# Decoder layer on one core: w_out and the feed-forward weights loaded into one shared ring of tiles, and the last units of the down projection finished one by one

## The chip, the cores and the metric

The kernel runs on one core of a Trainium2 chip. Times are microseconds of device time. Below, PE is TensorE, DVE is VectorE, ACT is ScalarE, POOL is GpSimd and SP is SyncE, which here only issues DMAs.

## What is computed

One layer of a hybrid decoder for 2112 tokens (64 sample tokens and 2048 prompt tokens), model width 1024, hidden width 2816, all in fp32:

```python
m = concat(rms_norm(gla(x @ w_in)) * silu(gate), rms_norm(gdn(x @ w_in)) * silu(gate)) @ w_out
x = layer_norm(ALPHA * x + m)
hid = silu(x @ w_ffn_gate) * (x @ w_ffn_up)
y = layer_norm(ALPHA * x + hid @ w_ffn_down)
```

`gla` and `gdn` are two recurrences over chunks of tokens, whose last states are outputs too.

## The kernel before

**Precision.** Every fp32 matmul of the large products is made as three: each operand is split into a rounded high part h and a rest l, and PE adds up h·h, h·l and l·h in PSUM. A split is an ACT cast (h) and a DVE subtraction (l).

**Stages.** phase_in projects x by w_in. The mixing (phase_gla, phase_gdn) runs the two recurrences, whose results go to device memory (`on_d` for the head outputs, `gt_d` for the gates). It ends at about 1108.5 us of the span. phase_out (L1038) follows, with 17 units: unit 0 has 64 tokens, units 1 to 16 have 128. Then comes the feed-forward: the gate and up products run over 3 blocks of 704 tokens and 22 weight slices f (until about 2285 us), the down projection over 5 groups of 4, 4, 3, 3 and 3 units and 22 slices each.

**One unit of phase_out** (`project`, L1054). For both head groups, `on` and `gt` are loaded, ACT sums the squares of `on` (L1066), POOL makes the factor, DVE scales, PE transposes `on` into PSUM `pt` (L1073: four 128x128 transposes), DVE multiplies by the gate (tile `gt`), ACT casts the high part `oh` (L1078), DVE makes the rest `ol`. Then 48 matmuls with 512 columns multiply by w_out (`gemm_t`, L249 to L251): 24 into one PSUM tile `pw` for the left 512 output columns, 24 into another for the right ones. DVE adds the residual out of PSUM (`xt`, L1088), a layer norm follows, PE transposes the result (`px`, L1094, two times four), ACT copies each half out of PSUM into the tile `x1T` (L1096) and issues its DMA to device memory itself (L1100). The pool has one buffer of `x1T` (`X1T = 1`), so that the second copy can only be made when the DMA of the first has landed.

**w_out before.** `load_quad` (L166 or so, called at the start of phase_out) loads w_out in eight DMAs of 512 KB through a staging tile `wraw` with two buffers. On each, DVE multiplies by the gain of the norm in place (L173), ACT casts the high part (L174), DVE subtracts. The parts stand in `o0h`, `o0l`, `o1h`, `o1l`.

**The feed-forward's weights before.** `load_pair` loads one slice of gate and up in one DMA of 1 MB into `wr` (two buffers), POOL makes three sums (`wt`), and seven splits go to `w` (nine pairs). The first call stands behind all of phase_out. `seven` multiplies in seven products p of 12 matmuls with 352 columns per half block. The down projection loads two slices per DMA into the same `wr`.

**Order of the work.** The kernel is written as if instructions ran in turn. A scheduler, which simulates a timeline when the program is built, then sets the order of the instructions on each engine, and inside an engine that order is kept on the chip. The program gives its hardware-queued DMAs eight landing semaphores in turn. So an edit in one place can move instructions of other places, and the order is read from the built program.

**End.** In the last group of the down projection (units 14 to 16, 18 matmuls per slice f and group), the loop over f is outside and the loop over units inside, so all three units end with the last slice, and their additions, layer norms and stores (L1210 to L1213) come behind PE's last matmul. The last unit's layer norm uses DVE for its last step, others ACT and POOL (`spare`).

Of the kernel before, what the change touches and what calls it, by code (L numbers as in the profile page):

```python
# [18 lines left out]
D = 1024  # L19
# [81 lines left out]
def hybrid_layer(ctx: ExitStack, tc: tile.TileContext, I, O):  # L101
# [25 lines left out]
    def vtt(out, a, b, op):  # L127
        nc.vector.tensor_tensor(out, a, b, op=op)  # L128
# [31 lines left out]
    c_G = cols.tile([64, 4], F32, name="c_G")  # L160
    flag = cols.tile([1, 1], mybir.dt.int32, name="flag")

    stg = ctx.enter_context(tc.tile_pool(name="stg", bufs=2))
    psg = ctx.enter_context(tc.tile_pool(name="psg", bufs=2, space=PSUM))

    def load_quad(pool, tag, src, gain):  # L166

        wh, wl = (pool.tile([128, 8, 512], F32R, name=tag + p, tag=tag + p, bufs=1) for p in "hl")
        v = src.rearrange("(k p) c -> p k c", p=128)
        for k in range(0, 8, 2):  # L170
            raw = stg.tile([128, 2, 512], F32, name="wraw", tag="wraw", bufs=2)
            nc.sync.dma_start(out=raw, in_=v[:, k:k + 2, :])
            nc.vector.tensor_scalar(raw, raw, gain[:, k // 4:k // 4 + 1], None, op0=TT.mult)  # L173
            nc.scalar.copy(wh[:, k:k + 2, :], raw)  # L174
            vtt(wl[:, k:k + 2, :], raw, wh[:, k:k + 2, :].bitcast(F32), TT.subtract)
        return wh, wl

# [17 lines left out]
    def sums(raw_x, r):  # L195

        r["S3"], r["S2"], r["S4"] = raw_x(), raw_x(), raw_x()
        ptt(r["S3"], r["11"], r["21"], TT.subtract)
        ptt(r["21"], r["21"], r["22"], TT.add)
        r["S1"] = r["21"]  # L200
        ptt(r["S2"], r["S1"], r["11"], TT.subtract)
        ptt(r["S4"], r["12"], r["S2"], TT.subtract)
        return r

    def load_pair(pw, src, plain=False):
# [40 lines left out]
    def gemm_t(out, wh, wl, xs, ts):  # L246

        for k in range(8):
            nc.tensor.matmul(out, lhsT=xs[0][k][:, ts], rhs=wh[:, k, :], start=(k == 0), stop=False)  # L249
            nc.tensor.matmul(out, lhsT=xs[0][k][:, ts], rhs=wl[:, k, :], start=False, stop=False)  # L250
            nc.tensor.matmul(out, lhsT=xs[1][k][:, ts], rhs=wh[:, k, :], start=False, stop=(k == 7))  # L251

# [15 lines left out]
    def phase_in(stack):  # L268
# [83 lines left out]
        for ib in range(3):  # L352
# [3 lines left out]
            for p in range(6):  # L356
# [680 lines left out]

    def phase_out(stack, ffn):  # L1038
        pi, po, p3 = (stack.enter_context(tc.tile_pool(reuse_waits=RW, name=n, bufs=2, side="right"))
                      for n in ("pi", "po", "p3"))  # L1040
        psm = stack.enter_context(tc.tile_pool(reuse_waits=RW, name="pso", bufs=2, space=PSUM))
        gain = pi.tile([128, 2], F32, name="gain", bufs=1)
        nc.sync.dma_start(out=gain, in_=I["norm_g"])
        wo = [load_quad(po, f"o{i}", I["w_out"][:, 512 * i:512 * i + 512], gain) for i in range(2)]
        lng = p3.tile([128, D], F32, name="lng", bufs=1)
# [8 lines left out]
        def project(u):  # L1054
# [53 lines left out]

    def phase_ffn(stack):
        NF = DFF // 128  # L1110
        pa = stack.enter_context(tc.tile_pool(reuse_waits=RW, name="pa", bufs=2))

# [34 lines left out]
        yield  # L1147
        pw = stack.enter_context(tc.tile_pool(reuse_waits=RW, name="pw", bufs=2, side="right"))
        p4 = stack.enter_context(tc.tile_pool(reuse_waits=RW, name="p4", bufs=2, side="right"))
        psp = stack.enter_context(tc.tile_pool(reuse_waits=RW, name="psp", bufs=6, space=PSUM))  # L1150

        for ib in range(3):
            xs = load_x1(ib) if ib else x_first
            for f in range(NF):
                kept = {}

                def done(j, i, t):
# [3 lines left out]
                    if (1 - j, i) in kept:  # L1161
# [14 lines left out]
        for nu in (4, 4, 3, 3, 3):  # L1176
# [8 lines left out]
            ys = {}  # L1185
            for f in range(NF):
                if f % 2 == 0:
                    raw = pw.tile([128, 4, 512], F32, name="wr")
                    nc.sync.dma_start(out=raw, in_=I["w_dn"][f // 2])
                wd = [part(pw, "w", 9, [128, 512], raw[:, 2 * (f % 2) + i, :], 512) for i in range(2)]  # L1190
                hr = p4.tile([128, 512], F32, name="hr")
                nc.sync.dma_start(out=hr[:, :T], in_=hid_d[f][:, c0:c0 + T])
                hh, hl = part(p4, "h", 3, [128, 512], hr[:, :T], T)
                if f == 0:
                    for u in us:
                        ys[u] = p4.tile([128, D], F32, name="y", bufs=5)
                        nc.sync.dma_start(out=ys[u][:units[u][1]], in_=x1_d[u])
                for u in us:
                    u0, C = units[u]
                    ts = slice(u0 - c0, u0 - c0 + C)  # L1200
                    for i in range(2):
                        p = ps[u, i][:C]
                        nc.tensor.matmul(p, lhsT=hh[:, ts], rhs=wd[i][0], start=f == 0, stop=False)  # L1203
                        nc.tensor.matmul(p, lhsT=hh[:, ts], rhs=wd[i][1], start=False, stop=False)  # L1204
                        nc.tensor.matmul(p, lhsT=hl[:, ts], rhs=wd[i][0], start=False, stop=f == NF - 1)  # L1205
            for u in us:
                u0, C = units[u]
                for i in range(2):
                    sl = slice(512 * i, 512 * i + 512)
                    nc.vector.scalar_tensor_tensor(ys[u][:C, sl], ys[u][:C, sl], ALPHA, ps[u, i][:C],  # L1210
                                                   op0=TT.mult, op1=TT.add)
                layer_norm(p4, ys[u], C, lng, lnb, spare=u < 16)
                ST.dma_start(out=O["y"][u0:u0 + C, :], in_=ys[u][:C])  # L1213
        yield

    def finish(rest):
        ffn = phase_ffn(rest)
        with ExitStack() as stack:
            phase_out(stack, ffn)
        next(ffn)  # L1220
# [21 lines left out]

GT, X1T = 3, 1
DEEPEST = 24.0
PBK = {"sc": 1, "inv": 2, "seq": 2, "po": 1}
# [61 lines left out]
```

## Time and profile before

| what | us |
|---|---|
| median of three runs | 2833.39 |
| lowest and highest run | 2832.21, 2848.49 |
| the profiled execution | 2829.82 |
| its span in the profile | 2827.7 |
| PE busy in the span | 2665.6 (94%) |
| DVE, ACT, POOL busy | 1982.8, 1241.3, 1176.9 |

The span goes from the first to the last recorded instruction of the profiled execution; 2.1 us lie around it. Stretches named below are microseconds from the start of the span. PE's busy share is an average: idle time of PE stands in the mixing, in the first 35 us of phase_out, at the change to the feed-forward, and at the end. The granted clock (PEclk) is the share of full speed that TensorE's clock had; 1.00 is 2.4 GHz, 0.50 is 1.2 GHz.

### The profile page before, as it was taken

How to read it: one execution, taken by the hardware profiler on the slowest of the kernel's cores; microseconds unless marked ns; L12 is line 12 of the kernel's file. 1: busy time of each engine (PE TensorE's matmuls, PEld its weight loads, DVE VectorE, ACT ScalarE, POOL GpSimd, SP SyncE). 2: the span in 40 equal slices, each digit the busy share in tenths (PEclk: the TensorE clock that was granted, in tenths of full speed). 3: DMA queues.
4: the chain of work that ended last, by engine and by line, in shares of the span. 5: the costliest groups of instructions: out<-in, count | busy, mean ns of one | idle time of the engine just before them, and what ended most of it. 6: DMA issues, size and time to landing. Idle time of an engine off the chain costs nothing.

```text
span 2827.7 us, 45495 instructions
## 1 busy us (share of the span) xinstructions
PE 2665.6 (94%) x16362; PEld 2435.2 (86%) x16362; DVE 1982.8 (70%) x3160; ACT 1241.3 (44%) x2660; POOL 1176.9 (42%) x1185
## 2 busy tenths in 40 slices
PE   8999999997888887999799999999999999999996
PEld 8999999995767675777799999999999987887885
DVE  7868768655678766686677788777877743555664
ACT  5545445434455553343344453444444432334442
POOL 6534325324344431354555559655665500210111
PEclk9999999996899998999899999999999999999998
DMA  7345344324533223667732346323432243536652
GB/s 258 126 152 186 121 144 157 108 101 126 148 98 99 65 70 102 188 205 240 239 117 101 112 147 203 114 101 124 140 107 103 100 144 131 202 131 244 214 200 85
DMA packets 244232, 406.60 MB, mean 144 GB/s; under 512 B 27900, under 2 KB 202460, under 8 KB 223132
## 3 DMA queue, kind: packets, MB, share of 16 engines
q1 hardware_dynamic: 195900, 364.22, 39.0%
q10 hardware_dynamic: 48096, 39.38, 4.2%
q8 instruction: 131, 2.15, 0.3%
q14 instruction: 105, 0.86, 0.1%
HBM read 305.01 MB, written 98.51 MB: 143 GB/s over the span
## 4 chain that ended last, share of the span: by engine, by line
PE 48%; DMA 2%; DVE 2%; POOL 1%; issue 1%; ACT 0%; SPq 0%; POOLq 0%; ACTq 0%; DVEq 0%
PE p L227 10%; PE p L228 10%; PE p L226 10%; PE p L1203 4%; PE p L1205 4%; PE p L1204 4%; PE g L1203 2%; PE g L1205 2%; PE g L1204 2%; DMA x1T<-x1T 1%; DMA xr<-x1T 1%; POOL xr L131 1%; DVE xl L128 0%; DMA wr<-in_w_dn 0%; DVE wl L128 0%
## 5 line engine op out<-in xcount | busy, mean ns | idle before, releaser
L128 DVE TENSOR_TENSOR wl<-wr,wh 128x512 fp32r<-128x512 f32 x652 | 595.1, 916 | 337.8 <-ACT wh L182 335.4
L226 PE MATMUL p<-xh,wh 128*128 128x352 f32 x2520 | 814.3, 323 | 10.2 <-ACT x1T L1096 5.0
L227 PE MATMUL p<-xl,wh 128*128 128x352 f32 x2520 | 815.1, 323 | 4.1 <-DVE xl L128 4.1
L228 PE MATMUL p<-xh,wl 128*128 128x352 f32 x2520 | 814.4, 323 | 0.3 <-DVE wl L128 0.3
L182 ACT CAST wh<-wr 128x512 fp32r<-128x512 f32 x652 | 401.1, 620 | 582.1 <-PE p L227 274.8
L226 PEld LDWEIGHTS p<-xh,wh 128*128 128x128 f32 x2520 | 474.6, 188 | 11.6 <-ACT x1T L1096 5.4
L227 PEld LDWEIGHTS p<-xl,wh 128*128 128x128 f32 x2520 | 474.8, 188 | 5.9 <-DVE xl L128 5.6
L228 PEld LDWEIGHTS p<-xh,wl 128*128 128x128 f32 x2520 | 474.8, 188 | 0.8 <-DVE wl L128 0.8
L128 DVE TENSOR_TENSOR t<-t,p 128x352 f32<-128x352 f32 x630 | 318.7, 518 | 199.0 <-PE p L228 197.3
L131 POOL TENSOR_TENSOR wt<-wr 128x512 f32<-128x512 f32 x180 | 243.9, 1355 | 242.8 <-DVE wl L128 211.7
L182 ACT CAST wh<-wt 128x512 fp32r<-128x512 f32 x270 | 167.5, 621 | 311.7 <-PE p L227 280.5
L1028 POOL TENSOR_SCALAR mv<-mv 128x1 f32<-128x1 f32 (+1 forms) x34 | 22.8, 674 | 505.6 <-DVE mv L1027 505.6
L128 DVE TENSOR_TENSOR wl<-wt,wh 128x512 fp32r<-128x512 f32 x270 | 202.7, 751 | 19.0 <-ACT wh L182 15.8
L1203 PE MATMUL p<-wh,hh 128*128 128x512 f32 x528 | 208.8, 395 | 0.0
L1204 PE MATMUL p<-wl,hh 128*128 128x512 f32 x528 | 208.7, 395 | 0.0
L131 POOL TENSOR_TENSOR wt<-wr,wt 128x512 f32<-128x512 f32 x90 | 119.4, 1326 | 212.2 <-DVE wl L128 212.0
L1205 PE MATMUL p<-wh,hl 128*128 128x512 f32 x528 | 204.5, 395 | 0.0
L316 PE MATMUL p<-xh,wh 128*128 128x352 f32 x576 | 186.2, 324 | 10.9 <-ACT xh L182 10.9
L317 PE MATMUL p<-xl,wh 128*128 128x352 f32 x576 | 186.3, 323 | 0.0
L318 PE MATMUL p<-xh,wl 128*128 128x352 f32 x576 | 186.2, 323 | 0.0
L131 POOL TENSOR_TENSOR t<-t 128x352 f32<-128x352 f32 x132 | 159.5, 1210 | 59.4 <-ACT t L93 35.3
L332 DVE SCALAR_TENSOR_TENSOR cv<-hb,cw,cv 128x352 f32<-128x352 f32 (+1 forms) x216 | 153.3, 715 | 40.2 <-ACT cv L330 22.6
(280 smaller groups left out, 4816.1 us busy)
## 6 DMA issues: line engine op xcount, KB each, us to landing
wr<-in_w_gu SPq DMA_DIRECT2D x66, 1024.0 KB, 4.9
wr<-in_w_dn SPq DMA_DIRECT2D x55, 1024.0 KB, 4.9
wr<-in_w_p SPq DMA_DIRECT2D x42, 1024.0 KB, 5.1
hid<-t SPq DMA_DIRECT2D x132, 176.0 KB, 1.8
xr<-in_xT SPq DMA_DIRECT2D x96, 176.0 KB, 4.6
dq<-cv ACTq DMA_DIRECT2D x72, 176.0 KB, 2.9
xr<-x1T SPq DMA_DIRECT2D x72, 176.0 KB, 3.6
hr<-hid SPq DMA_DIRECT2D x66, 192.0 KB, 3.4
```

The costliest lines, as they stand in the source:

```text
L128: nc.vector.tensor_tensor(out, a, b, op=op)
L131: nc.gpsimd.tensor_tensor(out, a, b, op=op)
L182: nc.scalar.copy(h[:, :N], raw)
L226: nc.tensor.matmul(ps, lhsT=h[:, ks], rhs=x[k][0], start=k == 0, stop=False)
L227: nc.tensor.matmul(ps, lhsT=h[:, ks], rhs=x[k][1], start=False, stop=False)
L228: nc.tensor.matmul(ps, lhsT=l[:, ks], rhs=x[k][0], start=False, stop=k == 3)
L316: nc.tensor.matmul(ps, lhsT=h(k), rhs=x[k][0], start=n == 0, stop=False)
L317: nc.tensor.matmul(ps, lhsT=h(k), rhs=x[k][1], start=False, stop=False)
L318: nc.tensor.matmul(ps, lhsT=l(k), rhs=x[k][0], start=False, stop=n == 7)
L1203: nc.tensor.matmul(p, lhsT=hh[:, ts], rhs=wd[i][0], start=f == 0, stop=False)
L1204: nc.tensor.matmul(p, lhsT=hh[:, ts], rhs=wd[i][1], start=False, stop=False)
L1205: nc.tensor.matmul(p, lhsT=hl[:, ts], rhs=wd[i][0], start=False, stop=f == NF - 1)
```

## The change

One ring of 34 tiles of 128x512 (`slot`, tag `o`), opened ahead of phase_out at the left end of memory, takes the place of `wraw` (for w_out), `o0h` to `o1l`, `wr`, `wt` and `w`. `RING = 34` and `LAST = 3` are new constants.

- w_out comes in 16 DMAs of 256 KB, all called ahead of the splits. A split is an ACT multiplication by the gain (128x512, high part) and a DVE scalar_tensor_tensor (raw times gain, less the high part). The gain is loaded in phase_in.
- A slice of gate and up comes in four DMAs of 256 KB (`ring_pair`), as do two slices of the down projection (`load_four`).
- The first slice of gate and up is called by the last unit of phase_out ahead of its layer norm (`next(ffn)` at `u == NU - 1`).
- The pool `pa` closes behind gate and up, and a pool `pd` opens for the down projection, with 6 pairs of `h` (before: 3) and 7 tiles `y` (before: 5).
- In each group of the down projection, slices 0 to 18 run as before; the last three run unit after unit, each followed by that unit's addition, layer norm and store.

The operations of phase_in, of the mixing and of `project` are otherwise the same.

```diff
+    def slot(ring, dt=F32):
+        return ring.tile([128, 512], dt, name="o", tag="o", bufs=RING)
+
+    def split(ring, raw):
+        h, l = slot(ring, F32R), slot(ring, F32R)
+        nc.scalar.copy(h, raw)
+        vtt(l, raw, h.bitcast(F32), TT.subtract)
+        return h, l
+
+    def load_four(ring, src):
+        raw = [slot(ring) for _ in range(4)]
+        for i in range(4):
+            nc.sync.dma_start(out=raw[i], in_=src[:, i, :])
+        return raw
+
+    def ring_pair(ring, src):
+        a1, a2, b2, b1 = load_four(ring, src)
...
+        return {n: split(ring, r) for n, r in zip(XO, (a1, t2, a2, b1, t3, b2, t4))}
...
                     if ib == 0:
...
+                        nc.sync.dma_start(out=gain, in_=I["norm_g"])
...
-        wo = [load_quad(po, f"o{i}", I["w_out"][:, 512 * i:512 * i + 512], gain) for i in range(2)]
+        raws = [[slot(ring) for _ in range(8)] for _ in range(2)]
+        for i in range(2):
+            for k in range(8):
+                nc.sync.dma_start(out=raws[i][k], in_=I["w_out"][128 * k:128 * k + 128, 512 * i:512 * i + 512])
+        wo = []
+        for i in range(2):
...
+            for k in range(8):
+                wh.append(slot(ring, F32R))
+                wl.append(slot(ring, F32R))
+                g = gain[:, k // 4:k // 4 + 1]
+                nc.scalar.mul(wh[k], raws[i][k], g)
+                nc.vector.scalar_tensor_tensor(wl[k], raws[i][k], g, wh[k].bitcast(F32), op0=TT.mult, op1=TT.subtract)
...
+            if u == NU - 1:
+                next(ffn)
             layer_norm(p3, xt, C, lng, lnb)
...
         x_first = load_x1(0)
         yield
+        w_first = ring_pair(ring, I["w_gu"][0])
+        yield
...
-                seven(p4, psp, load_pair(pw, I["w_gu"][f]), xs, done)
+                seven(p4, psp, ring_pair(ring, I["w_gu"][f]) if ib + f else w_first, xs, done)
...
+        first.close()
+        pd = stack.enter_context(tc.tile_pool(reuse_waits=RW, name="pd", bufs=2))
...
-                    raw = pw.tile([128, 4, 512], F32, name="wr")
-                    nc.sync.dma_start(out=raw, in_=I["w_dn"][f // 2])
-                wd = [part(pw, "w", 9, [128, 512], raw[:, 2 * (f % 2) + i, :], 512) for i in range(2)]
+                    raw = load_four(ring, I["w_dn"][f // 2])
+                wd[f] = [split(ring, raw[2 * (f % 2) + i]) for i in range(2)]
...
-                for u in us:
+                if f < NF - LAST:
+                    for u in us:
+                        down(u, f)
             for u in us:
+                for f in range(NF - LAST, NF):
+                    down(u, f)
...
                 layer_norm(pd, ys[u], C, lng, lnb, spare=u < 16)
                 ST.dma_start(out=O["y"][u0:u0 + C, :], in_=ys[u][:C])
+RING, LAST = 34, 3
```

The built program shows how instructions move. First SP, at the end of the mixing (its last store is `out_pgdn`) and the start of phase_out; `on_1` is the head output of unit 1, `gt` the gates. Before:

```order
189 L172 DMA wraw<-in_w_out 128x2x512 x2
190 L1047 DMA lng<-in_ln 128x1024
191 L1048 DMA lnb<-in_ln 128x1024
192 L172 DMA wraw<-in_w_out 128x2x512
193 L1018 DMA out_pgdn<-S 128x4x128
194 L172 DMA wraw<-in_w_out 128x2x512
195 L1059 DMA on<-on_1_72 128x512
196 L1059 DMA on<-on_1_89 128x512
197 L172 DMA wraw<-in_w_out 128x2x512
198 L1061 DMA gt<-gt 128x4x128 x2
199 L172 DMA wraw<-in_w_out 128x2x512 x2
```

After:

```order
195 L1034 DMA out_pgdn<-S 128x4x128
196 L1086 DMA on<-on_1_72 128x512
197 L1086 DMA on<-on_1_89 128x512
198 L1088 DMA gt<-gt 128x4x128
199 L1061 DMA o<-in_w_out 128x512 x16
200 L1086 DMA on<-on_2_73 128x512
201 L1088 DMA gt<-gt 128x4x128
202 L1086 DMA on<-on_2_90 128x512
203 L1088 DMA gt<-gt 128x4x128
```

In the second piece, after the change, the 16 loads stand together, behind the store `out_pgdn`, the two `on` of unit 1 and one `gt`; in the first, two of the eight loads stand ahead of that store and the others between `on` and `gt`.

Next ACT, in the middle of phase_out, from one unit's `x1T` copies to the next unit's casts. Before, then after:

```order
1291 L1096 COPY x1T<-px 128x512
1292 L1100 DMA x1T_135<-x1T 128x4x128
1293 L1078 CAST oh<-gt 128x512
1294 L1096 COPY x1T<-px 128x512
1295 L1100 DMA x1T_135<-x1T 128x4x128
1296 L1066 ACTIVATE misc,ssq<-on 128x128 x4
1297 L1078 CAST oh<-gt 128x512
1298 L1066 ACTIVATE misc,ssq<-on 128x128 x4
```

```order
1291 L1125 COPY x1T<-px 128x512
1292 L1129 DMA x1T_135<-x1T 128x4x128
1293 L1125 COPY x1T<-px 128x512
1294 L1129 DMA x1T_135<-x1T 128x4x128
1295 L1105 CAST oh<-gt 128x512
1296 L1093 ACTIVATE misc,ssq<-on 128x128
1297 L1105 CAST oh<-gt 128x512
1298 L1093 ACTIVATE misc,ssq<-on 128x128 x7
```

Before, a cast `oh` of the next unit stands between the two copies `x1T`; after, both copies and both DMAs stand ahead of both casts. All boundaries from unit 3 on repeat this.

Last PE at the same boundaries, from the last matmuls of a unit to the first of the next. Before, then after:

```order
7943 L251 MATMUL pw<-o1h,ol 128x512
7944 L249 MATMUL pw<-o1h,oh 128x512
7945 L250 MATMUL pw<-o1l,oh 128x512
7946 L251 MATMUL pw<-o1h,ol 128x512
7947 L1073 MATMUL pt<-ident,on 128x128 x4
7948 L249 MATMUL pw<-o0h,oh 128x512
7949 L250 MATMUL pw<-o0l,oh 128x512
7950 L251 MATMUL pw<-o0h,ol 128x512
```

```order
7884 L264 MATMUL pw<-o,oh 128x512
7885 L265 MATMUL pw<-o,oh 128x512
7886 L266 MATMUL pw<-o,ol 128x512
7887 L1100 MATMUL pt<-ident,on 128x128 x8
7888 L264 MATMUL pw<-o,oh 128x512
7889 L265 MATMUL pw<-o,oh 128x512
7890 L264 MATMUL pw<-o,oh 128x512
7891 L265 MATMUL pw<-o,oh 128x512
```

Before, four transposes `pt` stand at the boundary, those of the next unit's second head group; those of its first group, which its first 12 matmuls need, stand half a unit earlier. After, all eight transposes of the next unit stand behind the last matmul of the old one. Between the eight `px` and these eight `pt` stand 11 to 13 matmuls at eleven boundaries (12 or 13 at ten of them), 19 and 22 at two, and at the first, into unit 3, 9 behind the first four `px` and 2 behind the other four.

## Rows read from the trace of the kernel before

**Rows 1.** Windows of four stretches, every engine: w_out, units, change to feed-forward, down.

```profile
core 0: us, PE busy (x) PEld busy (x) DVE busy (x) ACT busy (x) POOL busy (x), PEclk, DMA share, GB/s
1108.50:1141.70 33.20, 19.67 (x71) 10.32 (x69) 23.02 (x34) 16.85 (x54) 11.08 (x12) 0.74 0.66 204
1141.70:1363.50 221.80, 211.61 (x1013) 170.11 (x1012) 161.91 (x230) 89.47 (x313) 102.62 (x120) 0.98 0.71 216
1363.50:1389.50 26.00, 11.47 (x39) 10.18 (x39) 14.89 (x15) 8.05 (x15) 13.70 (x10) 0.67 0.78 257
2285.00:2800.50 515.50, 515.23 (x2206) 407.37 (x2205) 270.09 (x402) 184.63 (x331) 58.17 (x42) 1.00 0.50 174
```

**Rows 2.** Timeline of PE, 1106 to 1142 (start, length, engine, line, [idle before <-releaser]).

```profile
1113.00 0.69 PE L1073 MATMUL pt<-ident,on 64*128 64x64 f32 x4 [4.33 <-DVE on L128]
...
1135.79 0.69 PE L249 MATMUL pw<-o1h,oh 128*64 128x512 f32 x1 [3.87 <-ACT o1h L174]
...
1141.65 0.45 PE L249 MATMUL pw<-o0h,oh 128*128 128x512 f32 x1
```

**Rows 3.** The w_out staging tile wraw: issue durations min/median/max, first and last start.

```profile
L172 SPq DMA_DIRECT2D wraw<-in_w_out x8: 368/373/384, 1076.0 to 1130.5; - x8
```

**Rows 4.** What PE waited for, 1142 to 1364: total, times, longest.

```profile
PE pw L249 <- ACT oh L1078: 4.4, 2, 4.0
PE pw L249 <- DVE xt L1088: 3.1, 2, 2.8
PE pt L1073 <- issue: 2.0, 1, 2.0
```

**Rows 5.** Timelines of PE, then ACT, then DVE, at one unit boundary.

```profile
1203.25 1.03 PE L1094 MATMUL px<-ident,xt 128*128 128x128 f32 x8
1204.05 0.48 PE L249 MATMUL pw<-o1h,oh 128*128 128x512 f32 x1
...
1205.53 0.60 PE L1073 MATMUL pt<-ident,on 128*128 128x128 f32 x4
...
1203.89 0.59 ACT L1096 COPY x1T<-px 128x512 f32<-128x512 f32 x1 [0.47 <-PE px L1094]
1204.51 0.37 ACTq L1100 DMA_DIRECT2D x1T<-x1T  x1
1207.34 0.62 ACT L1078 CAST oh<-gt 128x512 fp32r<-128x512 f32 x1 [2.87 <-DVE gt L128]
1209.04 0.59 ACT L1096 COPY x1T<-px 128x512 f32<-128x512 f32 x1 [1.07 <-DMA x1T<-x1T]
...
1210.12 0.31 ACT L1066 ACTIVATE misc<-on 128x128 f32<-128x128 f32 x1 [0.50 <-ACT x1T L1096]
...
1206.63 0.68 DVE L128 TENSOR_TENSOR gt<-gt,pt 128x512 f32<-128x512 f32 x1
```

**Rows 6.** The tile x1T, 1142 to 1364: its DMAs from issue to landing.

```profile
DMA to landing us min/median/max: 3.3/4.4/5.8
```

**Rows 7.** Windows of PE just behind three of its idle gaps: PE busy, granted clock.

```profile
1238.10:1242.50 4.40, 4.40 (x12) 0.62 0.86 254
1260.10:1263.50 3.40, 3.40 (x9) 0.57 0.23 55
1325.60:1332.00 6.40, 5.82 (x29) 1.00 0.96 315
```

**Rows 8.** Timeline of PE from the last transposes to the second product.

```profile
1368.77 1.90 PE L1094 MATMUL px<-ident,xt 128*128 128x128 f32 x8 [5.22 <-DVE xt L1035]
1374.71 0.66 PE L226 MATMUL p<-xh,wh 128*128 128x352 f32 x1 [4.03 <-ACT wh L182]
...
1384.21 0.66 PE L226 MATMUL p<-xh,wh 128*128 128x352 f32 x1 [4.97 <-ACT x1T L1096]
```

**Rows 9.** PE's last matmul, then SP's last DMA issue.

```profile
2803.59 0.40 PE L1205 MATMUL p<-wh,hl 128*128 128x512 f32 x1
...
2818.53 0.33 SPq L1213 DMA_DIRECT2D out_y<-y  x1
```

More of the change, by code (lines that the diff above doesn't have):

```diff
@@ L161, in hybrid_layer @@
     flag = cols.tile([1, 1], mybir.dt.int32, name="flag")
+    gain = cols.tile([128, 2], F32, name="gain")
     stg = ctx.enter_context(tc.tile_pool(name="stg", bufs=2))
     psg = ctx.enter_context(tc.tile_pool(name="psg", bufs=2, space=PSUM))
[L166 to L176, printed above, removed]
     def part(pool, tag, bufs, shape, raw, N):
@@ L203, in sums @@
         return r
+    def slot(ring, dt=F32):
[12 more added lines that the diff above has]
+        a1, a2, b2, b1 = load_four(ring, src)
+        t3, t2, t4 = (slot(ring) for _ in range(3))
+        ptt(t3, b2, b1, TT.subtract)
+        ptt(b1, b1, a1, TT.subtract)
+        ptt(t2, b2, b1, TT.subtract)
+        ptt(t4, a2, t2, TT.subtract)
+        return {n: split(ring, r) for n, r in zip(XO, (a1, t2, a2, b1, t3, b2, t4))}
     def load_pair(pw, src, plain=False):
@@ L248, in gemm_t @@
         for k in range(8):
-            nc.tensor.matmul(out, lhsT=xs[0][k][:, ts], rhs=wh[:, k, :], start=(k == 0), stop=False)
-            nc.tensor.matmul(out, lhsT=xs[0][k][:, ts], rhs=wl[:, k, :], start=False, stop=False)
-            nc.tensor.matmul(out, lhsT=xs[1][k][:, ts], rhs=wh[:, k, :], start=False, stop=(k == 7))
+            nc.tensor.matmul(out, lhsT=xs[0][k][:, ts], rhs=wh[k], start=(k == 0), stop=False)
+            nc.tensor.matmul(out, lhsT=xs[0][k][:, ts], rhs=wl[k], start=False, stop=False)
+            nc.tensor.matmul(out, lhsT=xs[1][k][:, ts], rhs=wh[k], start=False, stop=(k == 7))
     def keep(pool, po, C, dst):
@@ L1106, in phase_out, with phase_ffn @@
                 next(ffn)
-    def phase_ffn(stack):
+    def phase_ffn(stack, ring):
         NF = DFF // 128
-        pa = stack.enter_context(tc.tile_pool(reuse_waits=RW, name="pa", bufs=2))
+        first = ExitStack()
+        pa = first.enter_context(tc.tile_pool(reuse_waits=RW, name="pa", bufs=2))
         def raw_x():
@@ L1184, in phase_ffn, with down @@
                                 psp.tile([128, 512], F32, name="p", tag="p"))
-            ys = {}
+            ys, wd, hs = {}, {}, {}
+            def down(u, f):
+                u0, C = units[u]
+                ts = slice(u0 - c0, u0 - c0 + C)
+                hh, hl = hs[f]
+                for i in range(2):
+                    p = ps[u, i][:C]
+                    nc.tensor.matmul(p, lhsT=hh[:, ts], rhs=wd[f][i][0], start=f == 0, stop=False)
+                    nc.tensor.matmul(p, lhsT=hh[:, ts], rhs=wd[f][i][1], start=False, stop=False)
+                    nc.tensor.matmul(p, lhsT=hl[:, ts], rhs=wd[f][i][0], start=False, stop=f == NF - 1)
@@ L1192, in phase_ffn @@
+                hr = pd.tile([128, 512], F32, name="hr")
                 nc.sync.dma_start(out=hr[:, :T], in_=hid_d[f][:, c0:c0 + T])
-                hh, hl = part(p4, "h", 3, [128, 512], hr[:, :T], T)
+                hs[f] = part(pd, "h", 6, [128, 512], hr[:, :T], T)
                 if f == 0:
                     for u in us:
-                        ys[u] = p4.tile([128, D], F32, name="y", bufs=5)
+                        ys[u] = pd.tile([128, D], F32, name="y", bufs=7)
                         nc.sync.dma_start(out=ys[u][:units[u][1]], in_=x1_d[u])
-                for u in us:
[L1199 to L1205, printed above, removed]
+                if f < NF - LAST:
+                    for u in us:
+                        down(u, f)
@@ L1216, in finish @@
     def finish(rest):
-        ffn = phase_ffn(rest)
+        ring = rest.enter_context(tc.tile_pool(reuse_waits=RW, name="po", bufs=2))
+        ffn = phase_ffn(rest, ring)
         with ExitStack() as stack:
-            phase_out(stack, ffn)
+            phase_out(stack, ffn, ring)
         next(ffn)
```

13 lines of the change are left out of this document (5 added, 8 removed).

## The prediction

> **What bounds the kernel now.** I read the windows by stage first, then the waits of PE within a stage, then the timelines around them. PE sets the time nearly everywhere: in the middle of phase_out it is busy 211.61 of 221.80 us, in the down projection 515.23 of 515.50 [rows 1]. The change leaves PE's matmuls as they are, so it can win only where PE stands idle or at half clock. Three such places lie in its reach. At the start of phase_out PE is busy 19.67 of 33.20 us at a granted clock of 0.74 [rows 1]: it waits 4.33 us for `on`, later 3.87 us for a cast of w_out, and begins unit 1 only at 1141.65 [rows 2]. At the change to the feed-forward it is busy 11.47 of 26.00 us at 0.67 [rows 1], with gaps of 5.22, 4.03 and 4.97 us [rows 8]. At the end PE stops at 2803.59 + 0.40 = 2803.99 while the last store is issued at 2818.53 [rows 9] and the span ends at 2827.7. In between, one stage has little to give and much to lose: from 1142 to 1364 PE's three listed waits sum to only 4.4 + 3.1 + 2.0 = 9.5 us over 16 units [rows 4].
>
> **The start of phase_out.** What goes: eight loads of 512 KB that take turns in two buffers, the last issued at 1130.5 [rows 3]. What comes: 16 loads of 256 KB with a buffer each. They are called "ahead", but on SP they stand behind `out_pgdn`, both `on` of unit 1 and a `gt`, each of which waits for a buffer that unit 0 still uses. Unit 0's transposes can't come before the mixing's last matmul at about 1108.5, and behind them stand gate, cast and rest of unit 0 (each some 0.65, as the rows `gt` and `oh` show [rows 5]), with hand-overs about 3 us, so I put the loads at about 1112. 4.19 MB at 204 to 257 GB/s (the two stretches around [rows 1]) take 16.3 to 20.5 us: the last piece lands at 1128 to 1133. An ACT multiplication and a DVE operation of 512 columns follow (by their nearest rows 0.62 and 0.68 [rows 5]), so w_out is ready at about 1130 to 1134, and by then PE has done 12 matmuls of unit 1 (2.8 us) between those of unit 0. Unit 1 thus begins the equivalent of 7 to 13 us before 1141.65; other traffic shares the queues, so I take 10, with 5 and 13 as ends.
>
> The skill speaks against this part: the Trainium skill, page "DMA: Bandwidth & Descriptors", section "Bandwidth", asks for at least 1 MiB per DMA. By its fit of 2.0 us plus bytes over 436 GB/s a piece of 256 KB costs an estimated 2.6 us, 16 in turn 42 us, and the first term would be a loss of some 14 us. The page measures one DMA at a time; in this trace the rates above come with several in flight, and no row shows them in turn, so the sum does not use this.
>
> **The unit boundaries: the term that speaks against the change.** Before, the cast `oh` that the next unit's first matmuls need stands on ACT between the two `x1T` copies, and its transposes stand half a unit ahead. After, both transposes `pt` come behind the unit's last matmul, and both copies and both DMAs come ahead of `oh` on ACT. The second copy must wait for the landing of the first DMA, as there is one buffer. The rows of before show this chain whole [rows 5]: `px` done and PE going on at 1204.05, first copy 1203.89, DMA issued 1204.51, second copy only at 1209.04 (released by the DMA), next ACT operation at 1210.12. Put `oh` there: 1210.12 + 0.62 = 1210.74, that is 6.7 us after 1204.05. Before, nobody on PE needed that slot, as `oh` had run at 1207.34.
>
> After, PE has 12 or 13 matmuls at ten of the boundaries to fill this time, and eight `pt`. A matmul of 512 columns takes 515.23 / 2206 = 0.234 us [rows 1]; eight transposes take 1204.05 - 1203.25 = 0.80 us [rows 5]. That is 3.6 to 3.8 us, so PE stalls 2.9 to 3.1 us per boundary. With 11 matmuls it is 3.3; at the first, by the same count with 7 + 2 matmuls, about 3.6. The two with 19 and 22 matmuls fall to another floor: behind the last matmul DVE must evict (as long as `gt`, 0.68), multiply `gt` (0.68) and ACT cast (0.62), some 2.2 us with hand-overs against 0.8 of transposes, 1.4 us. Sum: 12 x 3.0 + 2 x 1.4 = 39 us. The landing of `x1T` took 3.3 to 5.8 us, median 4.4 [rows 6], and the stall follows it one for one: 12 x 1.9 + 2.8 = 26 us at the least, 12 x 4.4 + 2.8 = 56 at the most; were the DMA off the path altogether, the DVE floor gives 14 x 1.4 = 20. Against that stand the 9.5 us of waits which the old order had, and which go with it.
>
> The clock comes on top. Two of the old waits, of 2.8 and 4.0 us [rows 4], were followed by windows at 0.62 and 0.57 [rows 7], that is 2.4 GHz fallen to 1.2 for most of the window; the gap of 2.0 us was followed by 1.00 [rows 4, 7]. The price: (1 - 0.62) x 4.40 = 1.7 us and (1 - 0.57) x 3.40 = 1.5 us. Those 3.2 us go with the old waits. Stalls of 3.0 us lie at the edge of what these rows show, so I take half of the 12, 6 x 1.7 = 10 us, with 0 and 20 as ends. Net for this stage: 39 + 10 - 9.5 - 3.2 = +36 us; ends 20 - 12.7 = +7 and 56 + 20 - 12.7 = +63.
>
> **The change to the feed-forward.** The first slice's loads and splits move ahead of the last layer norm, so the wait of 4.03 us for a cast `wh` goes. Next late is the wait of 4.97 us for the last `x1T` copies, which the second product needs because its PSUM bank was theirs [rows 8]. That chain stays; it only gets less traffic beside it. Gain 0 to 5, taken 3.5. In steady gate, up and down work PE is the bound and covers smaller DMAs and the new order of splits; I cost that at nothing, and 5 us either way if the cover has holes. The mixing and phase_in keep their operations but are reordered in places: nothing, 5 either way.
>
> **The end.** Units now end 18 x 0.234 = 4.2 us apart. Behind the last matmul only one unit remains: on DVE an eviction and a statistics pass of 512 columns (each as `gt`, 0.68 [rows 5]), an aggregate, the root on POOL (which may still hold the addition of the unit before), and a DVE step of 1024 columns (twice that). With hand-overs I estimate 5 to 6.5 us to the last store's issue, where 2818.53 - 2803.99 = 14.5 us were needed [rows 9]. The 9.2 us behind the issue stay. Gain 8 to 9.5, taken 9.
>
> **Sum.** -10 + 36 - 3.5 - 9 = +13.5 us on the profiled execution of 2829.82, so about 2843.5. The median of the runs shown is 2833.39, 3.6 above that execution; on it the forecast is 2847. A measurement of this kernel tells about 1% (28 us) from no change, so this is no change that can be told.
>
> **The rivals.**
> 1. The boundaries cost little. If `x1T` lands early or the wait is hidden in a way that I don't see, only the DVE floor of 20 us stays, net +7, and the gains at 10 + 3.5 + 9 = 22.5 win: -15, 2818; with the upper ends of the gains (13 + 5 + 9.5) and 5 us from the reordered stages, 2808; with no stall at all, 2833.4 - 22.5 - 12.7 = 2798. For it: the DMA's landing varies by 2.5 us. Against it: ACT's order is fixed and the wait of the second copy is in the trace.
> 2. Slower: each boundary loses its clock too, and landing stays above the median, because PE's stall also delays `xt` and `on` loads into the same moments. At a landing of 5.4 us the stalls are 12 x 4.0 + 2.8 = 51, with 12 x 1.7 = 20 of clock and -12.7 the stage is +58, against 22.5: +36, 2869. It is slower by over 1% as soon as stall and clock exceed 28 + 22.5 + 12.7 = 63 us. For it: the clock fell behind gaps of 2.8 us. Against: the median landing gives 39.
> 3. The loads do come ahead: if they were issued in the mixing, w_out would cost PE no idle time and the first term could double to 20: 2837. SP's order speaks against it.
>
> **Chances.** Forecast (boundaries near the median, 2820 to 2861) 0.55; rival 1 0.20; rival 2 0.22; rival 3 0.03. Of rival 1 a good part ends within 1%, but my list of gains may be too short, so faster by over 1% gets 0.18; slower by over 1% 0.24; within 1% 0.58. Range 2804 to 2872: it leaves out the no-stall case and the worst landings.
>
> **What would show it.** Right, if PE's waits in phase_out name ACT `oh` some 14 times with 2.9 to 3.1 us each and ACT's own wait there is `x1T` for its DMA, if the w_out loads start near 1112 in a bunch, unit 1 starts some 10 us earlier, and the span ends about 15 us behind PE's last matmul. Wrong, if a unit's period stays near the old 13 us (221.80 us for some 17 units), if w_out is loaded before 1108, or if PE waits in the steady feed-forward.

## The result, and the profile after

The changed kernel takes 2952.32 us (median of 4 runs, 2938.41 to 2961.0) against 2834.26 of the kernel before: a ratio of 1.0405, 95% interval 1.0364 to 1.0445. That is 118 us slower, where no change was forecast and 2872 us was the upper end of the range. The profiled execution took 2961.0 us, its span is 2959.2.

The windows of PE by stage in the changed kernel (us, PE busy and matmuls, granted clock, DMA share, GB/s): mixing, phase_out up to the first product, gate and up, down, end.

```profile
core 0: us, PE busy (x), PEclk, DMA share, GB/s
642.00:1124.00 482.00, 408.05 (x3599) 0.84 0.32 91
1124.00:1445.10 321.10, 250.51 (x1088) 0.86 0.61 183
1445.10:2431.30 986.20, 911.92 (x5547) 0.98 0.35 112
2431.30:2943.10 511.80, 511.23 (x2244) 1.00 0.56 186
2943.10:2959.20 16.10, 0.00 (x0) 0.63 0.27 104
```

Two of the same stages in the kernel before, phase_out and gate and up, in the same columns:

```profile
1108.70:1374.70 266.00, 233.07 (x1088) 0.94 0.71 218
1374.70:2279.20 904.50, 893.91 (x5544) 0.99 0.37 127
```

Set side by side (borders: the same first and last matmuls), the 131.5 us between the two spans come from three places:

| stage | before | after | difference | of it PE idle |
|---|---|---|---|---|
| phase_in | 645.0 | 642.0 | -3.0 | |
| mixing | 463.7 | 482.0 | +18.3 | -0.7 |
| phase_out | 266.0 | 321.1 | +55.1 | +37.7 |
| gate, up and down | 1429.3 | 1498.0 | +68.7 | |
| of these gate and up | 904.5 | 986.2 | +81.7 | +63.7 |
| of these down | 524.8 | 511.8 | -13.0 | |
| end | 23.7 | 16.1 | -7.6 | |

So gate and up lost 81.7 us and down gained 13.0. The gain in down isn't idle time: before, 2206 of its matmuls took 515.50 us at a granted clock of 1.00 [rows 1], 0.234 us each, and after, 2244 took 511.80 us, 0.228 each. In the timelines they start every 0.233 us before and every 0.227 us after, and so it is in every run: down takes 511 to 515 us in all the kernels with the ring, 525 to 527 in all with the old tiles. The forecast didn't have this gain; no run shows what makes it.

The mixing's 18 us are no work of the change: with the same matmuls PE was busy 389.1 us before and 408.0 after, at a granted clock of 0.89 and 0.84. In two experiments below (runs 3 and 7), whose matmuls of the mixing stand in the changed kernel's order, this stage took 462 us; here the row of run 7:

```profile
641.80:1103.30 461.50, 383.54 (x3600) 0.90 0.33 95
```

Over all profiles of this study, the stage took 461.5 to 482.0 us, the shortest at a granted clock of 0.90, the longest at 0.84. Runs 6 and 11, whose instructions stand in the same order, differ in it by 6 us. I take it for scatter of the clock and leave it out of the account.

**phase_out.** What PE waited for between 1142 and 1434 us (total, times, longest), answering to [rows 4]:

```profile
PE pw L264 <- ACT oh L1105: 50.0, 14, 5.8
PE pw L266 <- DVE ol L128: 2.7, 1, 2.7
```

One boundary of units, first ACT, then PE (answers to [rows 5]):

```profile
1243.84 0.59 ACT L1125 COPY x1T<-px 128x512 f32<-128x512 f32 x1 [6.62 <-PE px L1123]
1244.46 0.37 ACTq L1129 DMA_DIRECT2D x1T<-x1T  x1
1249.10 0.59 ACT L1125 COPY x1T<-px 128x512 f32<-128x512 f32 x1 [4.67 <-DMA x1T<-x1T]
1249.72 0.37 ACTq L1129 DMA_DIRECT2D x1T<-x1T  x1
1250.13 0.62 ACT L1105 CAST oh<-gt 128x512 fp32r<-128x512 f32 x1 [0.44 <-DVE mv L1043]
...
1250.80 0.67 PE L264 MATMUL pw<-o,oh 128*128 128x512 f32 x1 [2.70 <-ACT oh L1105]
```

The chain is the one forecast: first copy, its DMA, 4.6 us later the second copy, its DMA, then the cast `oh`, and 0.67 us behind the cast's start PE goes on after 2.70 us of idleness. The waits of 9.5 us of before have become 52.7. And PE's clock fell, which answers to [rows 7]: behind all 15 of these stalls (2.15 to 5.80 us) the granted clock of the next 3.7 us was 0.50 to 0.63. The first row is the window behind this stall (us, PE busy, granted clock), the other three are the blocks of gate and up, for below:

```profile
1250.80:1254.50 3.70, 3.70 (x9) 0.54 0.85 219
1443.50:1740.00 296.50, 293.70 (x1827) 0.99 0.33 105
1740.00:2093.00 353.00, 314.81 (x1879) 0.96 0.38 123
2093.00:2431.30 338.30, 304.97 (x1850) 0.97 0.33 106
```

**The start of phase_out.** The 16 loads of w_out start 2.3 us behind the mixing's last matmul (1124.0) and take 10.45 us to issue; ACT's first multiplication stands at 1134.33, behind unit 1's squares and casts:

```profile
1126.33 10.45 SPq L1061 DMA_DIRECT2D o<-in_w_out  x16
...
1134.33 6.23 ACT L1069 ACTIVATE o<-o,gain 128x512 fp32r<-128x512 f32 x10
```

Each piece landed 5.6 us after its issue (median). By 1153.6, some 15 of unit 1's matmuls were done, as if it had begun 26 us behind the mixing, against 33 before: a gain of 7.

**Gate and up.** Here lies most of the loss, and nothing of it was forecast. PE's waits from 1445 to 2432 us; before, they came to 5.3 us in this stage behind its first two products:

```profile
PE p L241 <- ACT o L200: 58.3, 33, 10.9
PE p L243 <- DVE o L128: 11.4, 15, 2.8
PE g L1226 <- ACT hh L171: 4.5, 1, 4.5
```

The blocks' windows above show where: block 0 takes 296.5 us (before 296.0), block 1 353.0 (305.0), block 2 338.3 (300.0). Blocks 1 and 2 lose in two ways. The rows below are the start of block 1, its rest, the start of block 2 and its rest (us, then busy time and instructions of PE, PEld, DVE, ACT and POOL, granted clock, DMA share, GB/s):

```profile
1740.00:1830.00 90.00, 68.40 (x384) 66.33 (x383) 66.07 (x89) 32.55 (x66) 59.12 (x46) 0.87 0.58 190
1830.00:2093.00 263.00, 246.41 (x1497) 240.19 (x1495) 179.40 (x260) 95.01 (x189) 137.34 (x103) 0.99 0.31 101
2093.00:2190.00 97.00, 79.75 (x470) 78.25 (x470) 68.70 (x97) 37.48 (x74) 48.12 (x36) 0.91 0.35 115
2190.00:2427.00 237.00, 225.22 (x1381) 220.13 (x1379) 162.00 (x234) 86.56 (x168) 128.20 (x97) 1.00 0.31 101
```

PE is idle for 38.9 us in the two starts and for 28.4 in the rest. In the starts the next block's x is loaded and split on the same queues, and the slices' loads stand about 20 us apart (1762.40, 1782.50, 1801.82). In a steady slice of block 1, SP does (start, length, DMAs):

```profile
1813.17 3.38 SPq L1196 DMA_DIRECT2D hid<-t  x2
1816.64 1.83 SPq L207 DMA_DIRECT2D o<-in_w_gu  x4
1827.69 3.39 SPq L1196 DMA_DIRECT2D hid<-t  x2
1831.17 1.82 SPq L207 DMA_DIRECT2D o<-in_w_gu  x4
```

and POOL:

```profile
1822.42 4.35 POOL L131 TENSOR_TENSOR o<-o 128x512 f32<-128x512 f32 x3 [6.22 <-DMA o<-in_w_gu]
1826.73 0.94 POOL L131 TENSOR_TENSOR t<-t 128x352 f32<-128x352 f32 x1
1827.61 1.76 POOL L131 TENSOR_TENSOR o<-o 128x512 f32<-128x512 f32 x1
1829.33 1.40 POOL L131 TENSOR_TENSOR t<-t 128x352 f32<-128x352 f32 x1
```

Follow it round: SP loads a slice at 1816.64. POOL waits for it until 1822.42, makes three of the four sums (4.35 us), then multiplies gate by up of an older slice (`t`), makes the fourth sum, and multiplies again until 1830.73. The two stores `hid` of these products are on SP until 1831.08, and only behind them stands the next load, at 1831.17. From load to load 14.53 us; a slice took 13.5 us in block 0 (296.5 / 22). Over the steady parts the loads stand 14.8 us apart in block 1 (17 slices from 1816.64 to 2069.02) and 14.5 in block 2 (18 from 2140.68 to 2402.46). In the middle of block 0 POOL does this instead:

```profile
1606.82 1.26 POOL L131 TENSOR_TENSOR t<-t 128x352 f32<-128x352 f32 x1 [4.97 <-DVE t L128]
1609.67 0.95 POOL L131 TENSOR_TENSOR t<-t 128x352 f32<-128x352 f32 x1 [1.59 <-ACT t L93]
1610.58 5.41 POOL L131 TENSOR_TENSOR o<-o 128x512 f32<-128x512 f32 x4
```

There, sums follow the multiplications without any wait, as the slice was loaded one turn earlier. Block 0 neither began nor ended so. Up to 1530 us POOL waited for loads there too (five waits, 31.1 us), and from 1650 us on five times more (19.3 us), at last with 14.6 to 15.4 us from sums to sums (1681.78, 1696.58, 1711.16, 1726.52). PE stayed busy on the slices made ahead and first waited for a cast behind 1700 us (2.8 us). So the lead was spent before block 1 began. How POOL waited in block 1:

```profile
POOL o L131 <- DMA o<-in_w_gu: 118.1, 19, 8.0
```

**The end.** PE's last matmul ends at 2943.1, DVE's last step starts at

```profile
2950.14 1.28 DVE L1051 SCALAR_TENSOR_TENSOR y<-y,mv,lnb 128x1024 f32<-128x1024 f32 x1 [0.76 <-POOL mv L131]
```

and the span ends 16.1 us behind PE; before, 23.7 [rows 9].

### The profile page after: what moved, and what is told of

It reads as the page before. It is cut to its first block, busy times and chain, and to the rows that moved or that the text cites. A ratio compares the mean times of both kernels' runs of the same rounds, so it can differ in the third digit from the quotient of the medians.

```text
span 2959.2 us, 46216 instructions
## 1 busy us (share of the span) xinstructions
PE 2706.0 (91%) x16362; PEld 2473.4 (84%) x16362; DVE 1959.0 (66%) x3160; ACT 1217.8 (41%) x2668; POOL 1169.0 (40%) x1185
## 3 DMA queue, kind: packets, MB, share of 16 engines
q8 instruction: 131, 2.15, 0.3%
## 5 line engine op out<-in xcount | busy, mean ns | idle before, releaser
L128 DVE TENSOR_TENSOR o<-o 128x512 fp32r<-128x512 f32 x682 | 595.2, 909 | 196.3 <-ACT o L200 154.4
L241 PE MATMUL p<-xh,o 128*128 128x352 f32 x1848 | 606.2, 328 | 58.4 <-ACT o L200 58.3
L243 PE MATMUL p<-xh,o 128*128 128x352 f32 x1848 | 592.0, 325 | 11.4 <-DVE o L128 11.4
L200 ACT CAST o<-o 128x512 fp32r<-128x512 f32 x682 | 397.6, 617 | 490.9 <-POOL o L131 304.8
L242 PE MATMUL p<-xl,o 128*128 128x352 f32 x1848 | 599.0, 324 | 0.0
L131 POOL TENSOR_TENSOR o<-o 128x512 f32<-128x512 f32 x264 | 367.5, 1392 | 346.8 <-DMA o<-in_w_gu 305.3
L241 PEld LDWEIGHTS p<-xh,o 128*128 128x128 f32 x1848 | 351.4, 190 | 69.2 <-ACT o L200 68.9
L243 PEld LDWEIGHTS p<-xh,o 128*128 128x128 f32 x1848 | 349.4, 190 | 16.0 <-DVE o L128 16.0
L242 PE MATMUL p<-xl,wh 128*128 128x352 f32 x672 | 216.7, 323 | 0.0
L243 PE MATMUL p<-xh,wl 128*128 128x352 f32 x672 | 216.6, 322 | 0.0
L241 PE MATMUL p<-xh,wh 128*128 128x352 f32 x672 | 216.3, 322 | 0.0
L1226 PE MATMUL p<-o,hh 128*128 128x512 f32 x528 | 206.1, 391 | 0.0
L1227 PE MATMUL p<-o,hh 128*128 128x512 f32 x528 | 206.1, 390 | 0.0
L331 PE MATMUL p<-xh,wh 128*128 128x352 f32 x576 | 185.4, 323 | 8.4 <-ACT xh L171 8.4
L333 PE MATMUL p<-xh,wl 128*128 128x352 f32 x576 | 186.2, 323 | 0.0
L332 PE MATMUL p<-xl,wh 128*128 128x352 f32 x576 | 186.1, 323 | 0.0
```

The lines of the kernel that those rows point to most:

```text
L131: nc.gpsimd.tensor_tensor(out, a, b, op=op)
L200: nc.scalar.copy(h, raw)
L241: nc.tensor.matmul(ps, lhsT=h[:, ks], rhs=x[k][0], start=k == 0, stop=False)
L242: nc.tensor.matmul(ps, lhsT=h[:, ks], rhs=x[k][1], start=False, stop=False)
L243: nc.tensor.matmul(ps, lhsT=l[:, ks], rhs=x[k][0], start=False, stop=k == 3)
L331: nc.tensor.matmul(ps, lhsT=h(k), rhs=x[k][0], start=n == 0, stop=False)
```

## The experiments

Theories: **A**, the boundary stalls come from the second `x1T` copy's wait. **B**, the gate and up loss comes from the ring's size: 34 tiles hold 1.6 slices. **D**, it comes from the loop of in-order queues shown above. Their rivals stand in the expectations. A stage's length is read from the profile of each run.

**Run 1, two tiles x1T** in the changed kernel.

```diff
-GT, X1T = 3, 1
+GT, X1T = 3, 2
```

> The changed kernel with two buffers of the tile x1T instead of one. Theory A (at a unit boundary the next unit's cast oh waits on ACT behind the second x1T copy, which waits for the landing of the first half's DMA): the copies go one after the other, PE's stalls for oh in phase_out fall from 45.6 us to the floor of DVE and ACT, some 14 x 1.4 = 20 us, the clock falls less often, and the stretch from unit 2 to the feed-forward gets 25 to 40 us shorter; the kernel 2912 to 2928. Rival (the stalls come from the transposes pt standing behind the last matmul, with the chain through DVE): they stay near 45 us and the kernel stays at 2940 to 2960. Either way the gate and up stage stays near 985 us.

2907.72 us, ratio to the kernel before 1.026 (1.0221 to 1.03): 45 us less than the changed kernel, a little more than expected. phase_out 280.4 us instead of 321.1; gate and up 988.6. PE's waits between 1129 and 1381:

```profile
PE pw L264 <- ACT oh L1105: 22.1, 14, 5.0
```

The waits for `oh` fall from 50.0 us to 22.1; most are 1.15 us, and the granted clock behind those is 1.00. PE is busy 235.4 us in the stage against 250.5: the other 15 us were the clock. Theory A holds for this part; the 22.1 us that are left belong to its rival, as run 6 shows.

**Run 2, raw tiles of their own** for gate and up in the changed kernel.

```diff
-        raw = [slot(ring) for _ in range(4)]
+        raw = [own.tile([128, 512], F32, name="rw", bufs=8) if own else slot(ring) for _ in range(4)]
...
-ring_pair(ring, I["w_gu"][f])
+ring_pair(ring, I["w_gu"][f], own)
```

> The changed kernel with eight tiles of their own, outside the ring, for the raw weights of gate and up (same DMAs of 256 KB); the ring keeps its 34 tiles for w_out, sums, splits and the down projection. Theory B (34 tiles hold 1.6 slices of 21, so a slice's load can't be issued before the products of the slice two ahead have set tiles free; after a block's change the load, the sums on POOL and the casts form a loop of 14.9 us where PE needs 13.4): with two slices of raw tiles the loads come a slice earlier, blocks 1 and 2 take some 305 us each as block 0 does, gate and up some 905 to 920 instead of 983, the kernel 2875 to 2890. Rival C (four DMAs of 256 KB behind the two stores hid on SP's queue, whatever the buffers): PE still waits for casts in blocks 1 and 2, gate and up stays over 960.

2878.56 us, 1.0131 (1.0099 to 1.0164): 74 us less. Gate and up 909.8 us, PE idle in it 15 us instead of 74. From 1750 to 2350 us POOL has no wait for a weight's DMA left (the changed kernel: 220.0 us in 37); it waits for PE to free tiles:

```profile
POOL o L131 <- PE p L243: 86.0, 32, 3.1
```

The DMAs are the same 256 KB and stand on SP behind the same stores, so rival C falls. One thing moved with the tiles: POOL now makes one sum behind each multiplication and the other two later, where the changed kernel makes three and then one. So the run shows that raw tiles outside the ring cure the stage, and not how much of the cure is the earlier load and how much the order.

**Run 3, LAST = 0** in the changed kernel, and **run 4, the new end alone** in the kernel before.

```diff
-RING, LAST = 34, 3
+RING, LAST = 34, 0
```

> The changed kernel with LAST = 0, that is without the unit-by-unit end of the down projection's groups. If that end gives what the trace of before let expect, the time from PE's last matmul to the end of the span goes back from about 14 us to about 23 and the kernel is 8 to 10 us slower than the changed one, 2946 to 2966 by its own profile; if it costs PE waits between groups, it is faster. The order of other stages can shift by a few us.

2947.76 us, 1.0409 (1.037 to 1.0448): the 8 to 10 us of the expectation don't show in the time, which can't be told from the changed kernel's, but the end takes 22.1 us instead of 16.1.

```diff
+                if f < NF - LAST:
+                    for u in us:
+                        down(u, f)
             for u in us:
+                for f in range(NF - LAST, NF):
+                    down(u, f)
```

> The kernel before, with the unit-by-unit end of the last three slices alone (its weights' tiles and its 3 pairs of h as before, so the last three slices hold all of h). Expected 2822 to 2828 if the end's gain of 8 to 10 us stands alone; 2834 to 2850 if the held tiles keep the next group's loads and splits back at the four group changes (a wait of PE of 3 to 6 us at each).

2830.6 us, 0.9983 (0.9967 to 1.0), between the two expectations. The end takes 17.5 us instead of 23.7, but down takes 526.9 instead of 524.8, with 2.2 us of PE's waits for the splits of `h` that before had none; runs 9, 10 and 12 have the same 526.9. So the new end is worth 6 us, of which the kernel before with its 3 pairs of `h` gives 2 back.

**Run 5, both cures** (runs 1 and 2 together).

> The changed kernel with both cures: two buffers of x1T and eight raw tiles of their own for gate and up. Theories A and B are of different stages, so their gains add: 2952 - 45 - 74 = 2833 (2825 to 2842). Phase_out should take some 280 us as with two x1T alone, gate and up some 910 as with the raw tiles alone, and the whole should be within 1% of the kernel before. If a common cause (the clock, DMA traffic) stood behind both, the sum would fall short and the kernel stay over 2850.

2839.5 us, 1.0005 (0.9984 to 1.0026). phase_out 280.5, gate and up 911.8: the two causes are separate and add up, and without them the loss is gone. It is gone on balance only: phase_out is still 14.5 us and gate and up 7.3 us longer than before, against some 10 us less in down and 8 at the end.

**Run 6, a third tile `on`** on top of run 5.

```diff
-                on = pi.tile([128, 512], F32, name="on", bufs=2)
+                on = pi.tile([128, 512], F32, name="on", bufs=3)
```

> As the run with both cures, and a third buffer of the tile on, with which the built program's PE order has the transposes of one head group half a unit ahead again at most boundaries (as before the change). If the 14 boundary stalls of 1.15 us that two x1T leave come from the transposes behind the last matmul, phase_out gets 8 to 16 us shorter than 280 and the kernel ends at 2815 to 2828, below the one before. If the chain through DVE binds anyway, phase_out stays at 280.

2813.84 us, 0.9912 (0.9883 to 0.9941): 0.9% faster than the kernel before. phase_out 256.6 us, 24 less than in run 5 where 8 to 16 were expected: with the transposes apart again, the 14 waits of run 1 go too.

**Run 7, the hid stores from POOL** in the changed kernel.

```diff
-                        ST.dma_start(out=hid_d[f][:, t0:t0 + FN], in_=h)
+                        nc.gpsimd.dma_start(out=hid_d[f][:, t0:t0 + FN], in_=h)
```

> The changed kernel, ring and all, with only the two hid stores of each slice issued from POOL, behind the multiplication that makes them, instead of SP. Theory D (in blocks 1 and 2 a loop of queues sets the period of some 14.7 us: load on SP, sums on POOL, the gate-times-up multiplications behind them on POOL, hid stores behind those on SP, next load behind those): the loop is cut, the loads are issued as soon as their tiles are free, blocks 1 and 2 take 300 to 310 us each, gate and up 905 to 925, the kernel 2875 to 2895. Theory B alone (the ring's tiles are not free earlier): gate and up stays at 970 to 990, the kernel at 2940 to 2960. POOL's own issue of DMAs adds up to 2 us per slice on an engine that is idle 45% of the stage.

2929.56 us, 1.035 (1.0314 to 1.0387), gate and up 965.8: between the two expectations. The loop is cut: from 1723 to 2390 us POOL waits 10.4 us for a weight's DMA in 4 waits, where the changed kernel in the same stretch has 240.8 us in 40. But PE's idle time in the stage only falls from 74 to 63 us, and it now waits for the last of the splits:

```profile
PE p L243 <- DVE o L128: 32.1, 20, 5.0
PE p L241 <- ACT o L200: 28.3, 7, 9.4
```

DVE makes seven splits in one row, 1.40 us each

```profile
1875.67 9.78 DVE L128 TENSOR_TENSOR o<-o 128x512 fp32r<-128x512 f32 x7
```

while POOL makes the next sums from

```profile
1879.01 4.70 POOL L131 TENSOR_TENSOR o<-o 128x512 f32<-128x512 f32 x3
```

on; in the changed kernel six such splits took 5.21 us (0.87 each) at 1919.29, with POOL idle for most of that time. SP's loads now wait for tiles of the ring, that is for these splits (1800 to 2050 us):

```profile
SPq L207 <- DVE o L128: 181.2, 29, 12.7
```

So theory D is right about POOL's wait and wrong as the whole cause: with the queue's order cured, the ring still ties loads to splits, and more than half of PE's idle time (36.5 of 63 us) lies in the starts of blocks 1 and 2, where it was 38.9 before the cure.

**Run 8, a ring of 36 tiles.** (`RING, LAST = 36, 3`)

> The changed kernel with a ring of 36 tiles instead of 34. Theory B: two tiles more let half of a slice's four raw loads go one product earlier, so a part of the loss goes: gate and up 940 to 975. Theory D: the order on SP's and POOL's queues decides, two tiles change little: 975 to 990. All other stages as with the change; phase_out near 320.

2950.52 us (2 runs), 1.0405 (1.0365 to 1.0446), gate and up 982.6. Two tiles more change nothing that can be told; theory B in the form "the more tiles, the earlier the load" isn't borne out at this size. Between 36 in one ring and run 2's 42 in two parts no run stands, and none has a larger ring with the loop cut as well.

**Runs 9, 10 and 12, parts in the kernel before**, each with run 4's end. Run 9 loads w_out as the change does, into tiles of its own.

```diff
+                raw = po.tile([128, 512], F32, name="wo_raw", bufs=4)
+                nc.sync.dma_start(out=raw, in_=I["w_out"][128 * k:128 * k + 128, 512 * i:512 * i + 512])
+                wh.append(po.tile([128, 512], F32R, name="wo_h", bufs=16))
+                wl.append(po.tile([128, 512], F32R, name="wo_l", bufs=16))
```

> The kernel before with the unit-by-unit end of the last three slices, and w_out loaded as the change does it (pieces of 256 KB, gain on ACT, one DVE operation per piece, gain loaded early) into tiles of its own, four raw tiles and 32 for the splits; the feed-forward's weights stay in their old tiles. In the changed kernel's trace unit 1 was reached 26 us behind the mixing's last matmul against 33 before. If that gain of 7 us belongs to this way of loading, the stage phase_out takes 258 to 262 us against 268 with the end alone, and the kernel 2820 to 2826. If it came only from all 16 raw tiles being free at once, four raw tiles give none of it and phase_out stays at 266 to 270.

2824.23 us, 0.996 (0.9941 to 0.9979); phase_out 259.8 against 268.1 in run 4. The new way of loading is worth some 8 us in its stage, with four raw tiles.

Run 10 has `X1T = 2` instead.

> The kernel before with the unit-by-unit end and two buffers of x1T, w_out and weights as before. There the second x1T copy held nothing up that PE waited for, with transposes half a unit ahead. Expected: phase_out 262 to 270 us, no gain beyond the 3 to 6 us of PE's few waits, the kernel 2824 to 2832. A gain of over 10 us would say that the wait on the x1T DMA cost the old order too.

2816.55 us, 0.9946 (0.9927 to 0.9966): missed, better than expected. phase_out takes 260.2, 8 us less than run 4. PE's two waits for `oh` in the stage, 5.3 us in run 4, are gone, which fits a second `x1T` copy that held something up in the old order too. At the change to the feed-forward PE's gaps are 5.23, 4.62 and 4.37 us in run 4 ([rows 8] has them before) and 5.22 and 1.63 in this run; the third stood behind phase_out's end.

Run 12 has the parts of runs 9 and 10 with two raw tiles.

> The kernel before with the unit-by-unit end, two buffers of x1T, and w_out loaded in pieces as the change does it with two raw tiles of its own; the feed-forward's weights in their old tiles, no ring. In the built program the transposes are staggered over the unit at most boundaries. If the parts add, phase_out takes 260 - 6 = 254 us (with 252 to 260 if two raw tiles serve the loading less well than four), the other stages as in the run with two x1T and the end, and the kernel 2808 to 2814, below both kernels. If the loading gains nothing with two raw tiles, 2814 to 2822.

2827.25 us, 0.9966 (0.9944 to 0.9988): missed. phase_out takes 270.1 us. PE has a gap of 6.85 us at 1174, waiting for the residual's addition (`xt`), that neither part has alone. Each edit moves the scheduler's order, and what parts gain can't simply be added.

**Run 11, the first slice's call put behind phase_out** again, in run 6.

> The run with three buffers of on, two of x1T and raw tiles of its own, but the first slice of gate and up is called behind phase_out instead of ahead of the last layer norm. Theory E: in the changed kernel the early call put seven DVE splits and four POOL sums in front of the last layer norm, so PE waited 9.0 us for the last px (5.2 before) and saved the 4.0 us wait for the first cast and most of the 5.0 us wait behind it. Then without it px comes some 4 us earlier and the first products some 6 to 9 later: 2 to 5 us slower, 2816 to 2819. If the early call gains nothing net, within 1 us or faster.

2809.77 us, 0.9921 (0.9902 to 0.994). The built program has the same order as run 6 on every engine, though the call is written elsewhere. So this is run 6 once more, and theory E wasn't tried. The trace fits its first half, no more: DVE puts splits of the first slice between the parts of the last layer norm, and PE waits 10.83 us for the last `px`, where it waited 5.22 before [rows 8]:

```profile
1364.06 1.21 DVE L128 TENSOR_TENSOR o<-o 128x512 fp32r<-128x512 f32 x1 [2.68 <-ACT o L200]
1365.19 0.68 DVE L1041 BATCH_NORM_STATS2 bs<-xt 128x6 f32<-128x512 f32 x1
1365.79 1.27 DVE L128 TENSOR_TENSOR o<-o 128x512 fp32r<-128x512 f32 x2
1366.99 0.20 DVE L1043 BATCH_NORM_AGGREGATE mv<-bs 128x2 f32<-128x12 f32 x1
```

## Why the prediction was wrong

- **Steady gate and up: the step that failed.** "In steady gate, up and down work PE is the bound and covers smaller DMAs and the new order of splits; I cost that at nothing". Gate and up took 81.7 us longer, with PE idle for 63.7 of them, more than half of the loss. The cover held only until the end of block 0. I looked at PE's bound, but not at what stands ahead of the next load on SP and POOL: in the steady parts of blocks 1 and 2 a loop of queues with a period of 14.5 to 14.8 us replaced PE's 13.5, and at the blocks' starts the loads came later still. Run 2 shows that the raw loads' place in the ring made it: with raw tiles of their own the stage takes 909.8 us. Run 7 shows that the loop of queues alone did not: cut, it leaves PE idle for 63 us. The same sentence had down at nothing too; down got 13.0 us shorter, by a cause that stays open.
- **The unit boundaries: right in mechanism, too small.** Forecast 39 us of stalls, measured 52.7; typical stalls were 2.7 us against 3.0, but five were 4.4 to 5.8. I let half of the stalls cost their clock; all of them did, and run 1 puts it at some 15 us against 10. The whole stage came to +55, where 36 - 10 - 3.5 = +22 was forecast. Run 1 shows the cause of the larger part, run 6 that of the rest: the transposes behind the last matmul.
- **The start of phase_out: right.** Loads at 1124 + 2.3 us, not ahead; gain 7 to 8 us where 10 was taken and 5 to 13 allowed. The Trainium skill, page "DMA: Bandwidth & Descriptors", section "Bandwidth", asks for 1 MiB per DMA, by a measurement of DMAs issued from GpSimd. Here, issued from SP, smaller pieces were no loss: all 16, several in flight, were in place some 16 us after the first issue (10.1 us to the last issue and 5.6 to its landing). The page's fit gives an estimated 42 us for them in turn.
- **The change to the feed-forward: near in size, mixed in mechanism.** The wait of 4.03 us went, as forecast. The one of 4.97 us, which the forecast kept, went too, and the wait for `px` ahead of them, which it didn't look at, grew from 5.22 to 9.0. In sum 14.2 us became 9.0: 5 gained, where 3.5 was taken. That the size fits is in part luck.
- **The end: right in mechanism, a little small.** Forecast 9 us (8 to 9.5), measured 7.6 between the two kernels and 6 by runs 3 and 4.
- **The mixing.** 5 us either way were allowed; 18 came in the one profile, from its clock.

Of the rivals none held. The slower one had the boundaries right (51 us of stalls and a clock lost at each), but put all its loss there. Still open is why blocks 1 and 2 did not get back the turn that block 0 won after 1530 us and lost before its end. The loads of the next block's x begin on SP at 1735.82, when the lead was spent, so they did not start the loss; what in the order of the queues did is not shown.

## What to carry to other kernels

When loads, arithmetic and stores of neighbouring steps share in-order queues, walk round the loop from one load to the next and compare its length with the bound engine's period; a buffer count alone doesn't show it. In run 2 staging tiles for raw loads, kept apart from the tiles of their products, gave the load its lead back. And one buffer too few on a small store (`x1T`) can hold up, through an engine's order, a cast that a busy PE needs at every step.

## What the runs showed of the hardware

TensorE's clock: in phase_out of the changed kernel all 15 stalls of 2.15 to 5.80 us were followed by 3.7 us at a granted clock of 0.50 to 0.63, most of it 1.2 GHz (0.54 in the window shown). Those of 1.15 us in run 1 were followed by 1.00, and PE's busy time in the stage was 15 us less for the same matmuls. DVE's splits of 512 columns took 0.87 us each in one burst, and 1.40 in another that ran beside POOL's additions (run 7); no run sets POOL apart as the cause. The matmuls of down with 512 columns started every 0.227 us in the kernels with the ring and every 0.233 in those with the old tiles, at a granted clock of 1.00 in both; why stays open. And the mixing, the same work in all these kernels, took between 461.5 and 482.0 us, at granted clocks of 0.90 and 0.84.
